# Moving the decays, the rings and the value loads of a two-layer encoder kernel

## The chip, the cores and the metric

The kernel runs on one core of one Trainium2 chip. The metric is device time in microseconds (us) of one execution; three executions of the kernel before are given below, and their median is what the prediction has to hit for the changed kernel. One further execution was recorded by the profiler, and every duration in this document that stands in a row comes from such a recorded execution.

## The reference

The program is one float32 encoder of two layers on 512 tokens of width 1024. Cut to what matters here:

```python
def _odd_mixer(x, norm_g, w_in, dec_f, dec_b, gn_g, w_out):
    h = _rmsnorm(x, norm_g)
    q, k, v, g = _split(h @ w_in, ODD_SPLITS)          # 1024, 1024, 2048, 2048 columns
    lgf = jax.nn.log_sigmoid(dec_f.astype(jnp.float32))   # 8 decays each way
    lgb = jax.nn.log_sigmoid(dec_b.astype(jnp.float32))
    y_f = _retention_dir(q, k, v, lgf, False)
    y_b = jnp.flip(_retention_dir(jnp.flip(q, 1), jnp.flip(k, 1), jnp.flip(v, 1), lgb, True), 1)
    ...                                                   # group norm per head -> yn
    return (jax.nn.silu(g) * yn) @ w_out

def reference(x, ...):
    for layer in range(DEPTH):
        x = x + (_even_mixer(x, ...) if layer % 2 == 0 else _odd_mixer(x, ...))
        x = x + _mlp(x, ...)                              # relu(h @ w1)**2 @ w2, 4096 wide
    return x
```

The even mixer is windowed attention with sinks beside neighbourhood attention on a grid. A retention head multiplies its scores by a decay per distance, `exp(log_gamma * distance)`; `log_gamma` is the log-sigmoid of 16 inputs.

## The kernel before, in words

Four stages follow each other on the one core: even mixer, first MLP, odd mixer, second MLP. Every float32 matmul is made of three products of rounded halves: an operand is split by a cast on ACT (the high part, `whi`, `shi`, `xh`, `uh`, `vh`) and a subtraction on DVE (the low part, `wlo`, `slo`, `xl`, `ul`, `vl`), and TensorE adds high·high, high·low and low·high. So each product waits for both a cast and a subtraction, and it can be late by either.

**Even mixer.** A scheduler with a cost model orders its instructions on every engine. Queries and keys are scaled by their norms (L464 on DVE; L460 and L465 on POOL), transposed by PE (L479), evacuated as high and low parts (L484, L494 on ACT, L485, L495 on DVE), and the window's scores (L635, L636 on PE) go through a fused minimum on DVE (L566) and an exponential on ACT (L576). `decays` (L1638) is called after the even mixer, and the scheduler is free to put its operations into gaps: they work on tiles of 128x16, most of them on POOL, and write `lg` and `nlb`, which the odd mixer reads some 600 us later.

**The MLPs and the odd mixer's values** are products of Strassen's kind. A *stream* is written in a fixed order for PE, DVE and ACT: at step k come the matmuls of block k, requests of weights (`ask`), the functions filed under `early[k]`, the cast of the weights of step k+2 (`high`, L1099), the functions under `mid[k]`, the subtraction for step k+2 (`low`, L1105), and those under `post[k]`. `request` (L1062) loads a block of 512 KB: blocks A12 and A22 into a ring of three (`wraw`), the others into a ring of six (`sraw`). S1 and S3 are sums of two blocks: SyncE's queue loads the first (L1068), and POOL issues an accumulating load of the second (L1070). `sum2` (L1077) makes S2 = A11 + S1 on DVE. `combine` (L999) makes the input sums of two of the eight row blocks: four operations on DVE into a tile `c` (L1009 to L1012), a cast `uh` (L1015), a subtraction `ul` (L1016).

**Start of the odd mixer.** The queries and keys of the first of four quarters are projected by `proj_a` (matmuls L186 to L188; its weights pass through the same ring `wraw`, with a cast L165 and a subtraction L166), evacuated by L1726 and L1731 and split by L1702 and L1703. Among that work stand the four `combine` calls, the first requests of the values' stream, and its first two `high` and `low`. The scheduler orders all of this too; only the stream behind it has a fixed order. The steps 0 and 1 of the stream take A11, 2 and 3 take S1, 4 and 5 S2, 6 and 7 A12, 8 and 9 S3; each is 12 matmuls of 512 columns (L1507 to L1509).

**Quarters.** Each of the four quarters has two heads. For quarter i: scores (L1788 to L1790), product with the decays (L1793), split into `ath`, `atl`, output (L1801 to L1803), then for each head the statistics of its group norm (cast L1819, subtraction L1820, two matmuls L1821 and L1822, then L1825 to L1827 on ACT and L1828, L1829 on DVE) and the gate (L1846, L1849, split into `zh`, `zl`), the output projection of the quarter before, and the projections of quarter i+1. In `project` each of the four value rows of the next quarter is loaded on ACT's queue (L1756) and split into `vh` (L1702) and `vl` (L1703). The scheduler orders this stage.

## Time and profile before

| what | value |
|---|---|
| three executions | 1300.21, 1300.35, 1302.45 us, median 1300.35 |
| profiled execution | 1302.67 us, of which 1300.9 us from the first to the last instruction (the span) |
| mean granted TensorE clock | 0.996 |
| busy, share of the span | PE 1277.1 us (98%), DVE 1055.0 (81%), ACT 825.6 (63%), POOL 152.2 (12%) |
| DMA | 196.15 MB, 151 GB/s over the span |

PE is busy nearly all the time, so what another engine does counts only where PE waits for it. A row of the waits reads: waiting engine, tile and line, then what it waited for, then total us, times, longest. A row of the timeline reads: start, duration, engine, line, operation, output and inputs, shape, count, and in brackets the idle time before it with what ended it. Matmuls overlap, so a row of PE is longer than its share: matmuls of 512 columns start 0.23 us apart at the full clock.

### The profile page before, as it was taken

To read this page: it belongs to the slowest core of one execution; us is meant where nothing else is said; L and a number is where in the kernel's file an instruction comes from. 1 tells how busy PE (TensorE), PEld (TensorE's weight loads), DVE (VectorE), ACT (ScalarE), POOL (GpSimd) and SP (SyncE) were. 2 spreads that over 40 slices of the span, in tenths; PEclk is the share of its full clock that TensorE was granted. 3 is DMA by queue.
4 is the path that set the end of the run, shared out by engine and by line. 5 is a ranking of instruction groups with operands and counts; after the bars stand their busy time and mean duration, and the time that the engine had idled before them with its cause. 6 is when DMAs were issued, how large, how long until landed. Compare 5 with 4: busy or idle time off the path is not lost.

```text
span 1300.9 us, 19400 instructions
## 1 busy us (share of the span) xinstructions
PE 1277.1 (98%) x7186; PEld 1117.9 (86%) x7186; DVE 1055.0 (81%) x1602; ACT 825.6 (63%) x1382; POOL 152.2 (12%) x169
## 2 busy tenths in 40 slices
PE   8899999999999999999999999999999999999998
PEld 7788978888989989887899977888888889898997
DVE  6588886959797997987888788877777787979888
ACT  4589875775766747675775566454547757566573
POOL 0322440001111101010110000000000111101100
PEclk9899999999999999999999999999999999999999
DMA  5222231758688686286899323415135777868862
GB/s 170 82 77 81 82 94 48 206 158 201 177 193 197 165 200 181 62 248 169 199 267 242 123 76 110 160 35 162 49 97 162 178 211 174 202 167 181 214 149 81
DMA packets 167072, 196.15 MB, mean 151 GB/s; under 512 B 12225, under 2 KB 124865, under 8 KB 166977
## 3 DMA queue, kind: packets, MB, share of 16 engines
q1 hardware_dynamic: 130384, 147.74, 36.7%
q0 software_dynamic: 27776, 37.75, 17.8%
q10 hardware_dynamic: 8816, 9.41, 2.3%
q8 instruction: 56, 0.92, 0.3%
q14 instruction: 40, 0.32, 0.1%
HBM read 184.39 MB, written 10.49 MB: 150 GB/s over the span
## 4 chain that ended last, share of the span: by engine, by line
PE 89%; DVE 5%; ACT 3%; DMA 1%; issue 1%; POOL 1%; SPq 0%; ACTq 0%; DVEq 0%; POOLq 0%
PE acc L1297 7%; PE acc L1298 7%; PE acc L1299 7%; PE acc L1313 7%; PE acc L1312 7%; PE acc L1314 7%; PE acc L186 7%; PE acc L188 6%; PE acc L187 6%; PE acc L1509 2%; PE acc L1508 2%; PE acc L1507 2%; PE aux L1297 1%; PE aux L1299 1%; PE aux L1298 1%
## 5 line engine op out<-in xcount | busy, mean ns | idle before, releaser
L1099 ACT CAST whi<-sraw 128x1024 fp32r<-128x1024 f32 x121 | 126.8, 1050 | 84.9 <-PE acc L1314 25.3
L1105 DVE TENSOR_TENSOR wlo<-sraw,whi 128x1024 fp32r<-128x1024 f32 x121 | 147.9, 1223 | 32.7 <-ACT whi L1099 32.2
L165 ACT CAST whi<-wraw 128x1024 fp32r<-128x1024 f32 (+2 forms) x83 | 78.4, 946 | 77.4 <-PE acc L187 38.8
L1070 POOL DMA_DIRECT2D sraw<-in_w_mlp_out_dram x32 | 38.7, 1236 | 625.9 <-DMA sraw<-in_w_mlp_out_dram 378.7
L166 DVE TENSOR_TENSOR wlo<-wraw,whi 128x1024 fp32r<-128x1024 f32 (+2 forms) x74 | 82.7, 1117 | 36.0 <-ACT whi L165 35.0
L186 PE MATMUL acc<-xh,whi 128*128 128x512 f32 x272 | 106.5, 392 | 0.0
L187 PE MATMUL acc<-xl,whi 128*128 128x512 f32 x272 | 106.1, 390 | 0.0
L188 PE MATMUL acc<-xh,wlo 128*128 128x512 f32 x272 | 105.6, 390 | 0.0
L1297 PE MATMUL acc<-uh,whi 128*128 128x256 f32 x344 | 97.8, 284 | 0.2
L1299 PE MATMUL acc<-uh,wlo 128*128 128x256 f32 x344 | 97.2, 283 | 0.0
L1298 PE MATMUL acc<-ul,whi 128*128 128x256 f32 x344 | 97.2, 283 | 0.0
L1099 ACT CAST shi<-sraw 128x1024 fp32r<-128x1024 f32 x59 | 62.1, 1052 | 38.8 <-PE acc L1314 10.7
L1105 DVE TENSOR_TENSOR slo<-sraw,shi 128x1024 fp32r<-128x1024 f32 x59 | 72.2, 1223 | 15.7 <-ACT shi L1099 15.4
L1266 DVE SCALAR_TENSOR_TENSOR rows<-acc,tok_r,rows 128x512 f32<-128x512 f32 (+1 forms) x97 | 71.8, 744 | 1.9 <-PE acc L1314 1.9
L1105 DVE TENSOR_TENSOR wlo<-wraw,whi 128x1024 fp32r<-128x1024 f32 x46 | 56.3, 1224 | 16.2 <-ACT whi L1099 16.2
L1297 PEld LDWEIGHTS acc<-uh,whi 128*128 128x128 f32 x344 | 65.6, 191 | 1.0 <-ACT s L1188 1.0
L1298 PEld LDWEIGHTS acc<-ul,whi 128*128 128x128 f32 x344 | 65.6, 191 | 0.0
L1299 PEld LDWEIGHTS acc<-uh,wlo 128*128 128x128 f32 x344 | 65.6, 191 | 0.0
L188 PEld LDWEIGHTS acc<-xh,wlo 128*128 128x128 f32 x272 | 51.0, 188 | 11.1 <-DVE wlo L166 0.4
L187 PEld LDWEIGHTS acc<-xl,whi 128*128 128x128 f32 x272 | 51.1, 188 | 10.5
L186 PEld LDWEIGHTS acc<-xh,whi 128*128 128x128 f32 x272 | 51.1, 188 | 10.5
L1099 ACT CAST whi<-wraw 128x1024 fp32r<-128x1024 f32 x46 | 48.3, 1051 | 12.5 <-PE acc L1314 8.9
(401 smaller groups left out, 4180.9 us busy)
## 6 DMA issues: line engine op xcount, KB each, us to landing
sraw<-in_w_mlp_out_dram SPq DMA_DIRECT2D x48, 512.0 KB
wraw<-in_w_mlp_in_dram SPq DMA_DIRECT2D x40, 512.0 KB
sraw<-in_w_mlp_in_dram SPq DMA_DIRECT2D x36, 512.0 KB
sraw<-in_w_mlp_out_dram POOLq DMA_DIRECT2D x32, 512.0 KB, 8.7
wraw<-in_w_mlp_out_dram SPq DMA_DIRECT2D x32, 512.0 KB
wraw<-in_w_in_o_dram SPq DMA_DIRECT2D x32, 512.0 KB
sraw<-in_w_mlp_in_dram POOLq DMA_DIRECT2D x24, 512.0 KB, 8.1
sraw<-in_w_in_o_dram SPq DMA_DIRECT2D x24, 512.0 KB
```

Of the source, the lines that this page charges most:

```text
L166: eng.tensor_tensor(lu, used, hu.bitcast(F32), op=ALU.subtract)
L186: mm(ps[m], hi[:, k % 4, cs], xh, start=k == 0, stop=False)
L187: mm(ps[m], hi[:, k % 4, cs], xl, start=False, stop=False)
L188: mm(ps[m], lo[:, k % 4, cs], xh, start=False, stop=k == nk - 1)
L1099: nc.scalar.copy(h, self.weight(k))
L1105: V.tensor_tensor(l, self.weight(k), h.bitcast(F32), op=ALU.subtract)
L1297: mm(o, h[:, i, cs], bh, start=st, stop=False, skip_group_check=True)
L1298: mm(o, h[:, i, cs], bl, start=False, stop=False, skip_group_check=True)
L1299: mm(o, l[:, i, cs], bh, start=False, stop=i == 3, skip_group_check=True)
L1312: mm(oc, bh[:, i, cs], hc, start=st, stop=False, skip_group_check=True)
L1313: mm(oc, bh[:, i, cs], lc, start=False, stop=False, skip_group_check=True)
L1314: mm(oc, bl[:, i, cs], hc, start=False, stop=end, skip_group_check=True)
```

## The change

Three edits, in the order of the program:

1. `decays` becomes a generator that is called in the first MLP's stream, at the steps 20 to 23, piece by piece. Two POOL operations become DVE operations; the clamped input goes into `lg` first.
2. In the values' stream the tile `c` no longer has a ring of its own (one slot) but takes slots in the ring `sraw` of six. The first requests are split: S1 and A11 after the second `combine`, A12 and then S3 after the projection of the keys. `sum2` of the first half is filed one step later.
3. The value rows of the next quarter are loaded by `load_v` right after both heads, and split by `split_v` after the first head's gate, no longer in `project`.

```diff
-        CB = ("c", 1)
-
...
             for q in range(2):
                 s = 14 * q
-                put(post, s - 2 if q else s, lambda q=q: self.sum2(2, q, 0))
-                put(post, s + 1, lambda q=q: self.sum2(2, q, 1))
+                put(post, s - 2 if q else s + 1, lambda q=q: self.sum2(2, q, 0))
+                put(post, s + 1 if q else s + 2, lambda q=q: self.sum2(2, q, 1))
...
     def decays():
         dx = hb[:, 8:24]
         u, s2, pl = ls
-        G.tensor_scalar(u, dx, -1.0, None, op0=ALU.mult)
-        V.tensor_tensor(u, u, dx, op=ALU.min)
+        V.scalar_tensor_tensor(u, dx, -1.0, dx, op0=ALU.mult, op1=ALU.min)
+        V.tensor_scalar(lg, dx, 0.0, None, op0=ALU.min)
+        yield
         act(u, u, AF.Exp)
-        G.tensor_scalar(s2, u, 2.0, None, op0=ALU.add)
+        yield
+        V.tensor_scalar(s2, u, 2.0, None, op0=ALU.add)
         V.reciprocal(s2, s2)
+        yield
         G.tensor_tensor(u, u, s2, op=ALU.mult)
...
-        V.tensor_scalar(u, dx, 0.0, None, op0=ALU.min)
         G.tensor_scalar(pl, pl, -2.0, None, op0=ALU.mult)
-        G.tensor_tensor(lg, pl, u, op=ALU.add)
+        G.tensor_tensor(lg, pl, lg, op=ALU.add)
...
                 if qt == 0:
                     values.combine(0)
-                    values.ask(-99, -2)
                     values.combine(1)
+                    values.ask(-99, -5)
                     values.combine(2)
                     values.combine(3)
                 proj_a(w_in_o, 0, 8, 1024 + qt * 256, xg, ev_k)
                 if qt == 0:
                     values.scales(rc)
-                    values.ask(-2, 0)
+                    values.ask(-2, 1)
+                    values.ask(-5, -2)
                     values.enter()
                     return
+                with tc.issue_after(mark):
+                    self.load_gates(nc.scalar)
+
+            def load_v(self):
+                self.back = []
                 for t in range(NB):
-                    r = row()
-                    with tc.issue_after(mark):
-                        if t == 0:
-                            self.load_gates(nc.scalar)
-                        nc.scalar.dma_start(r, scr[qt][t * P : (t + 1) * P, :])
-                    self.v[t] = split(r, "v", 4)
+                    self.back.append(row())
+                    with tc.issue_after(marks[-1]):
+                        nc.scalar.dma_start(
+                            self.back[t], scr[self.qt][t * P : (t + 1) * P, :]
+                        )
+
+            def split_v(self):
+                for t in range(NB):
+                    self.v[t] = split(self.back[t], "v", 4)
...
             q.head(0)
             q.head(1)
+            n and n.load_v()
             for c in range(2):
                 q.stats(c)
                 q.gate(c)
+                c == 0 and n and n.split_v()
                 p and p.output(4 * c, 4 * c + 4)
             n and n.project()
...
             st.enter()
+            if not last:
+                pieces = decays()
+                for k in range(20, 24):
+                    st.mid[k] = [lambda: next(pieces, None)]
...
     even_mixer(n_mlp0)
-    decays()
     mlp(0, n_mlp0(), n_odd)
```

The first place is POOL's list in the even mixer, before: the end of the first part of the decays (`ls`, `lg`, `nlb` are their tiles), scaling of queries (`qn`), a subtraction of weights, and the start of the second part.

```order
L1651 TENSOR_SCALAR ls_110<-ls_110 128x16
L1650 TENSOR_TENSOR ls_110<-ls_110,ls_109 128x16
L1651 TENSOR_SCALAR ls_110<-ls_110 128x16
L465 TENSOR_TENSOR qn<-raw,rs 128x4x64
L460 TENSOR_TENSOR qn<-raw,rs 128x512 x2
L166 TENSOR_TENSOR wlo<-wraw,whi 128x2x384
L465 TENSOR_TENSOR qn<-raw,rs 128x4x64
L1650 TENSOR_TENSOR ls_110<-ls_110,ls_109 128x16
L1651 TENSOR_SCALAR ls_110<-ls_110 128x16
```

In the changed kernel the same place of POOL's list reads:

```order
L96 TENSOR_SCALAR ngv<-gv 128x32
L465 TENSOR_TENSOR qn<-raw,rs 128x4x64
L460 TENSOR_TENSOR qn<-raw,rs 128x512 x2
L166 TENSOR_TENSOR wlo<-wraw,whi 128x2x384
L465 TENSOR_TENSOR qn<-raw,rs 128x4x64
L166 TENSOR_TENSOR wlo<-wraw,whi 128x2x384
```

The decays are gone from it (11 operations ahead of the first `qn` and 12 after the last), and so are three of them from DVE's list and one from ACT's; all other rows of the even mixer keep their order on PE, DVE, ACT and POOL.

The second place is SyncE's list at the start of the odd mixer, as a difference: `wraw ... 128x4x256` are the weights of the projections, `wraw` and `sraw ... 128x2x512` the blocks of the values' stream.

```order
 L144 DMA wraw<-in_w_in_o_dram 128x4x256 x4
+L1072 DMA wraw<-in_w_in_o_dram 128x2x512 x2
 L1068 DMA sraw<-in_w_in_o_dram 128x2x512 x2
 L1072 DMA sraw<-in_w_in_o_dram 128x2x512 x2
+L1072 DMA wraw<-in_w_in_o_dram 128x2x512
+L1068 DMA sraw<-in_w_in_o_dram 128x2x512 x4
```

The two blocks of A12 (`wraw`) moved ahead of S1 (L1068, `sraw`, two) and A11 (L1072, `sraw`, two), and S3 moved behind them. On DVE, at the same place, the second `low` of the values' stream (`wlo` of A11's second half, L1105) stood before like this:

```order
L1016 TENSOR_TENSOR ul_6288<-c_6282,uh_6287 128x1024
L1703 TENSOR_TENSOR ql_6271<-tmp_6268,qh_6270 128x512
L1703 TENSOR_TENSOR ql_6277<-tmp_6274,qh_6276 128x512
L1009 TENSOR_TENSOR c_6309<-row_6307 128x256
L1011 SCALAR_TENSOR_TENSOR c_6309<-xT3_6151,gv_76,row_6307 128x256
L1010 SCALAR_TENSOR_TENSOR c_6309<-xT3_6151,ngv_104,c_6309 128x256
L1105 TENSOR_TENSOR wlo_6424<-sraw_6299,whi_6423 128x1024
```

and in the changed kernel, from the first `low` (`slo`) on:

```order
L1105 TENSOR_TENSOR slo_6421<-sraw_6307,shi_6420 128x1024
L1016 TENSOR_TENSOR ul_6298<-c_6292,uh_6297 128x1024
L1016 TENSOR_TENSOR ul_6319<-c_6313,uh_6318 128x1024
L1009 TENSOR_TENSOR c_6324<-row_6322 128x256
L1011 SCALAR_TENSOR_TENSOR c_6324<-xT7_6158,gv_76,row_6322 128x256
L1010 SCALAR_TENSOR_TENSOR c_6324<-xT7_6158,ngv_104,c_6324 128x256
L1732 SCALAR_TENSOR_TENSOR tmp_6395<-acc_6333,rstd_b_6182 128x512
L1012 SCALAR_TENSOR_TENSOR c_6324<-xT7_6158,ngv_104,c_6324 128x256
L1732 SCALAR_TENSOR_TENSOR tmp_6401<-acc_6334,rstd_b_6182 128x512
L1704 TENSOR_TENSOR kl_6398<-tmp_6395,kh_6397 128x512
L1105 TENSOR_TENSOR wlo_6425<-sraw_6309,whi_6424 128x1024
```

That `low` moved from the second `combine` (`c_6309`) to behind the fourth (`c_6324`) and most of the evacuation of the keys.

The third place is PE's list between quarter 0 and quarter 1, where the statistics of head 1 (L1821, L1822; L1831, L1832 in the changed kernel) stand among the projection of quarter 1's queries. Before:

```order
L186 MATMUL acc_8241<-xh3_6057,whi_8244 128x512
L1821 MATMUL aux_8214<-ath_8215,ones_r_74 128x512
L187 MATMUL acc_8241<-xl3_6058,whi_8244 128x512
L188 MATMUL acc_8241<-xh3_6057,wlo_8245 128x512
L1822 MATMUL aux_8214<-atl_8216,ones_r_74 128x512
L186 MATMUL acc_8240<-xh4_6059,whi_8274 128x512
```

In the changed kernel:

```order
L1831 MATMUL aux_8237<-ath_8238,ones_r_74 128x512
L186 MATMUL acc_8263<-xh5_6060,whi_8297 128x512
L187 MATMUL acc_8263<-xl5_6061,whi_8297 128x512
L188 MATMUL acc_8263<-xh5_6060,wlo_8298 128x512
L186 MATMUL acc_8264<-xh5_6060,whi_8297 128x512
L187 MATMUL acc_8264<-xl5_6061,whi_8297 128x512
L188 MATMUL acc_8264<-xh5_6060,wlo_8298 128x512
L1832 MATMUL aux_8237<-atl_8239,ones_r_74 128x512
L186 MATMUL acc_8263<-xh6_6062,whi_8297 128x512
```

The second matmul of that pair is the 4305th of PE's list before and the 4317th now. The first matmul on the low part of the keys' weights (`wlo_8319` before, `wlo_8342` now) is the 4334th in both, so 29 matmuls stood between them and 17 do now. DVE makes that low part (L166) behind the same operations as before: what follows from the statistics (L1828, two `zl`, L1829).

## The prediction

> **What bounds the kernel now.** I read the page first, then the waits of PE, then the timelines around each wait, then the clock in windows.

> ```profile
> PE 1277.1 (98%) x7186; PEld 1117.9 (86%) x7186; DVE 1055.0 (81%) x1602; ACT 825.6 (63%) x1382; POOL 152.2 (12%) x169
> ...
> PE aux L635 <- DVE qk L485: 3.7, 1, 3.7
> ...
> PE acc L1508 <- DVE slo L1105: 2.0, 1, 2.0
> PE acc L186 <- ACT whi L165: 1.4, 1, 1.4
> ...
> PE acc L1509 <- DVE ul L1016: 1.0, 1, 1.0
> ...
> PE aux L1788 <- ACT kh L1702: 0.8, 1, 0.8
> ...
> PE aux L479 <- POOL qn L465: 0.3, 1, 0.3
> ```

> PE is the bound almost everywhere; it can only gain where it waits. The first five of these waits, at three places, are the ones that the three edits touch: one in the even mixer, two at the start of the values' stream, two between quarters 0 and 1. No matmul is removed. The third view shows what a wait costs beside its own length:

> ```profile
> 50.50:57.30 6.80, 5.66 (x21) 5.69 (x22) 4.92 (x12) 3.74 (x10) 0.00 (x0) 0.50 0.23 61
> ...
> 596.70:600.00 3.30, 3.30 (x9) 2.51 (x9) 1.70 (x2) 1.34 (x2) 1.59 (x2) 0.50 0.77 175
> 787.00:797.00 10.00, 8.31 (x35) 6.39 (x36) 9.76 (x16) 7.37 (x12) 0.00 (x0) 1.00 0.15 56
> ```

> The third figure from the right is the granted clock. It fell to half behind the wait in the even mixer, for 6.8 us, and behind the two of the values' stream (2.0 and 1.0 us, 2.3 us from one end to the other), for 3.4 us; behind the two between the quarters (0.8 and 1.4, 4.5 us from one end to the other) it stayed at 1.00. At half clock 3.4 us do the work of 1.7, so such a stretch costs 1.7 us more.

> **Edit 1, the decays.** What PE waits for in the even mixer is DVE, and DVE waits for POOL:

> ```profile
> 38.45 0.22 POOL L1646 TENSOR_TENSOR ls<-ls,ls 128x16 f32<-128x16 f32 x1 [0.93 <-DVE ls L1645]
> ...
> 41.34 0.62 POOL L465 TENSOR_TENSOR qn<-raw,rs 128x256 f32<-128x256 f32 x1
> ...
> 49.07 0.22 POOL L1652 TENSOR_TENSOR ls<-ls,ls 128x16 f32<-128x16 f32 x1
> ...
> 44.43 0.74 DVE L485 SCALAR_TENSOR_TENSOR qk<-aux,gq,qk 64x512 fp32r<-64x512 f32 x1 [0.25 <-ACT qk L484]
> 49.32 0.17 DVE L1653 TENSOR_SCALAR ls<-hb 128x16 f32<-128x16 f32 x1 [4.15 <-POOL ls L1652]
> ...
> 49.97 1.53 DVE L485 SCALAR_TENSOR_TENSOR qk<-aux,gq,qk 64x512 fp32r<-64x512 f32 x2
> ...
> 45.45 0.28 PE L636 MATMUL aux<-qk 128*128 128x256 f32 x1
> ...
> 47.65 0.34 PE L212 MATMUL acc<-whi,xl 128*128 128x384 f32 x1
> 51.64 0.55 PE L635 MATMUL aux<-qk 128*128 128x256 f32 x1 [3.65 <-DVE qk L485]
> ...
> 54.45 0.41 PE L635 MATMUL aux<-qk 128*128 128x256 f32 x1
> ...
> 57.39 0.33 PE L212 MATMUL acc<-whi,xl 128*128 128x384 f32 x1
> ```

> One tiny operation of the decays (L1653) sits in DVE's list ahead of the scores' minimum and the keys, and waits 4.15 us for POOL's polynomial. With it gone DVE takes the scores of 45.45 with L566 (0.5 us, from about 45.8) and L485 twice (1.5): done near 47.8, where PE comes to it at 47.8. POOL's chain from 38.45 no longer stands before L465 at 41.34, so PE's wait of 0.3 for it goes too, and PE and DVE both get there some 0.3 earlier, at 47.5. From 51.64 that is 4.1 us. The next L635, at 54.45, needs a fourth L485 (0.7) behind an L166 (1.0) on DVE: ready near 49.3, 5.1 us earlier than before, where PE would come without a wait near 48.9. From 54.45 to 57.39 PE runs 2.9 us at half clock; at the full clock it is 1.5 to 1.7. So the place of 57.39 comes at about 51.0: **-6.3 us**. Bounds: -3.7 if only the wait goes, -7.2 if the 0.4 at the fourth L485 doesn't come and PE gains 0.5 more ahead of it. I take the worked-out value, since the lists of PE and DVE are otherwise unchanged there.

> In the new place, the first MLP, the 21 POOL operations (nine of them take from 38.45 to 41.34, 0.32 us each: 6.7 us) stand between these two:

> ```profile
> 334.85 1.20 POOL L1070 DMA_DIRECT2D sraw<-in_w_mlp_out_dram  x1 [1.13 <-DMA sraw<-in_w_mlp_out_dram]
> 356.63 1.20 POOL L1070 DMA_DIRECT2D sraw<-in_w_mlp_out_dram  x1 [20.58 <-DMA sraw<-in_w_mlp_out_dram]
> ```

> 20.6 us idle cover them. The four operations on DVE and one on ACT (0.2 us each) lie in a stream where PE never waits: 0, and 1 us if that cover were gone.

> **Edit 2, the values' stream.** First what feeds it:

> ```profile
> 561.75 0.88 SPq L1068 DMA_DIRECT2D sraw<-in_w_in_o_dram  x2
> ...
> 564.95 9.56 SPq L1072 DMA_DIRECT2D wraw<-in_w_in_o_dram  x3
> ...
> 568.02 1.23 DVE L166 TENSOR_TENSOR wlo<-wraw,whi 128x1024 fp32r<-128x1024 f32 x1 [2.10 <-ACT whi L165]
> ...
> 564.00:588.00 24.00, 24.00 (x109) 19.79 (x108) 19.88 (x38) 16.61 (x26) 4.82 (x4) 1.00 1.07 292
> ```

> A12 takes slots of the ring that the projections' weights pass through; its second block can go out only when the L166 of 568.02 is done, at 569.2. In the changed queue S1 and A11 stand behind it: they go out at 569.2 and not from 561.75, 7.5 us later. At 292 GB/s a block of 512 KB takes 1.8 us. A12's second block, S1's two and A11's two are the first five, and S1's accumulating loads come between: A11's second block lands between 578.2 (five blocks) and 581.9 (seven), say 581.

> Then DVE. Its list behind the L166 of the last projection weights:

> ```profile
> 572.89 1.23 DVE L166 TENSOR_TENSOR wlo<-wraw,whi 128x1024 fp32r<-128x1024 f32 x1 [0.15 <-ACT whi L165]
> 574.03 1.28 DVE L1726 TENSOR_TENSOR tmp<-acc,rstd_b 128x512 f32<-128x512 f32 x2
> 575.23 1.22 DVE L1016 TENSOR_TENSOR ul<-c,uh 128x1024 fp32r<-128x1024 f32 x1
> 576.36 1.29 DVE L1703 TENSOR_TENSOR ql<-tmp,qh 128x512 fp32r<-128x512 f32 x2
> 577.56 0.42 DVE L1009 TENSOR_TENSOR c<-row 128x256 f32<-128x256 f32 x1
> ...
> 586.22 0.40 PE L1508 MATMUL acc<-wlo,xh 128*128 128x512 f32 x1
> ...
> 593.90 0.50 PE L1508 MATMUL acc<-slo,uh 128*128 128x512 f32 x1 [1.99 <-DVE slo L1105]
> ...
> 596.18 0.50 PE L1509 MATMUL acc<-shi,ul 128*128 128x512 f32 x1 [0.97 <-DVE ul L1016]
> ```

> From start to start: L166 and `low` 1.14, two L1726 1.20, L1016 1.13, two L1703 1.20; an operation of `combine` like L1009 0.4. Up to the first `low`: 1.14, 1.20, 1.13, 1.20, six operations of `combine` 2.4, `low` 1.13: done at 581.1. The second `low` then has two `ul` (2.3), four operations of `combine` (1.5), two evacuations and one `kl` (1.8) ahead of it, and itself 1.2: 587.9 at the earliest. The `uh` for the second `ul` stands on ACT behind the cast of A11's second block, so a landing at 581 adds about 0.7: 588.6. PE needs it at 586.22: a **new wait of 2.4 us**, and perhaps 0.2 on the next `low`. It is 1.7 without the landing, 4.8 if A11 lands 2.5 us later. What PE waited for at 593.90 and 596.18 (3.0 us) is not late any more, since three of the four `ul` are done before the stream's second step and PE comes 2.5 us later. A restart costs about 0.2 (an estimate: a row behind a wait is 0.50 long, the others 0.40, and the weights are loaded again). Lost before: 3.0, restarts 0.4, half clock 1.7: 5.1. Lost now: 2.6, restarts 0.4, and half clock 1.7 if a wait of this length brings it: 4.7. So **-0.4 us**, from -5.1 (no new wait at all) to +3.5 (the long one, and half clock twice).

> **Edit 3, the value rows.** The two waits between the quarters come from four casts `vh` on ACT that stand between `kh` and the weights:

> ```profile
> 782.23 2.15 ACTq L1756 DMA_DIRECT2D row<-values  x4
> ...
> 788.18 2.52 ACT L1702 CAST vh<-row 128x512 fp32r<-128x512 f32 x4 [0.31 <-DMA row<-values]
> ...
> 769.38 0.41 PE L1822 MATMUL aux<-atl,ones_r 128*128 128x512 f32 x1
> ...
> 774.90 1.22 DVE L166 TENSOR_TENSOR wlo<-wraw,whi 128x1024 fp32r<-128x1024 f32 x1
> ...
> 776.17 0.74 PE L188 MATMUL acc<-xh,wlo 128*128 128x512 f32 x2
> ```

> They move to the statistics, and both waits go: 2.2 and 0.4 of restarts, **-2.6 us**. The four loads move with them; their issue holds ACT for 2.2 us ahead of the last head's evacuation, where nothing of PE waits for it yet. But the casts and four `vl` of 0.6 on DVE push something too. Before, the chain from the second statistics matmul at 769.38 over ACT and DVE to the end of L166 at 776.1 takes 6.7 us, and 29 matmuls cover it (29 times 0.23 is 6.7): L188 at 776.17 comes just in time. In the changed list that matmul stands 12 later, near 772.15, and only 17 matmuls (3.9 us) cover the chain. Some 0.8 of the 6.7 were waits of ACT for a cast of weights and of DVE for a gate, so 5.9 are left: 772.15 + 5.9 is 778.05, needed at 776.05: a **new wait of 2.0 us**, at L188 for L166. It is nothing if the chain were hidden, 3.2 if the rows land late (they have 5 us from issue, as 782.23 to 788.18 took before) and the statistics matmul itself waits. Behind it `kl` and `ath` are late by 0.4 in sum, since another L166 stands between them on DVE. New: 2.0 + 0.4 + 0.4 of restarts, and half clock 1.7: **+4.5**. Net **+1.9 us**, from -2.6 to +3.5.

> **The clock.** The rows: 3.65 us of waiting brought half clock, 2.0 and 1.0 within 2.3 us brought it, 0.8 and 1.4 within 4.5 us did not. A single wait of 2.0 to 2.4 lies nearer to the second, so I count it both times. [...]

> **Sum.** -6.3 - 0.4 + 1.9 = **-4.8 us** against the profiled execution: 1302.67 becomes 1297.9, its span 1296.1. The median before is 2.3 us below the profiled execution, and I carry this over: 1300.35 - 4.8 = **1295.5**.

> **Rivals.**
> - *No half clock behind the new waits* (it seems to be counted over stretches of 3.4 us, and their border may cut a wait in two): -6.3 - 2.1 + 0.2 = -8.2, 1292.1. For: the full clock from 787 to 797. Against: 596.70. 0.22.
> - *At least one of the new waits isn't there.* Without that of edit 2 the sum is -6.3 - 5.1 + 1.9 = -9.5, without that of edit 3 -6.3 - 0.4 - 2.6 = -9.3, without both -14.0. So 1286.3 to 1291. For: DVE is busy 19.9 of the 24 us up to 588, so there is room. Against: the lists, which put the late operation last. 0.20.
> - *The gain of the even mixer is absorbed*: minimum, exponential and transposes, not PE, would set the pace behind 57, PE's waits there grow by what it gained, and -3.7 is left: sum -2.2, 1298.1. For: what PE waits for at 51.64 is such a chain. Against: no list is changed there. 0.15.
> - *Slower*: the requests behind A12 bring A11 so late that the stream starts dry. It decides when A11's second block lands at 587 and not 581: then the wait is 8.3 us with half clock twice, edit 2 costs +7.0, and the sum is +2.6, 1303. For: DMA is full up to 588. Against: only seven blocks are in the way. 0.04, and 0.03 for a weaker form that leaves no gain.
> - My forecast: 0.36, own range 1293 to 1298.

> A measurement tells 0.2% (2.6 us) from nothing. Faster, below 1297.75: the forecast but 0.01, the first two rivals, a third of the third: 0.82. Same: the rest of these and the weaker form of the last, 0.14. Slower: 0.04. The range that holds 8 in 10 is 1288.5 to 1298.5: it leaves out the case without both new waits and the late A11.

> **What would show it.** The wait of L635 gone and the clock 1.00 from 45 to 57; a wait L1506 or L1507 for `wlo` L1105 at the stream's second step, no wait for `slo` or `ul`; S1's requests behind a pause of SyncE; the waits at the first scores of quarter 1 and for `whi` gone, one of L188 for `wlo` L166 some 10 us before. I am wrong if the stream's second step starts without a wait, if the keys' L188 doesn't wait, or if the even mixer gives under 4 us.

## The result and the profile after

The changed kernel takes 1293.92 us (median of 1293.56, 1293.90, 1293.94 and 1295.38) beside 1300.28 us for the kernel before on the same chip: a ratio of 0.9949, 95% interval 0.9932 to 0.9967. Its profiled execution took 1295.38 us with a span of 1293.6, 7.3 us under that of before. Forecast were 1295.5 us, and 4.8 us less than before; measured are 6.4 us less between the medians and 7.3 between the profiled executions. The page's busy times and PE's waits of the changed kernel:

```profile
PE 1273.7 (98%) x7186; PEld 1115.5 (86%) x7186; DVE 1056.3 (82%) x1603; ACT 823.7 (64%) x1382; POOL 160.8 (12%) x167
...
PE acc L1506 <- DVE wlo L1105: 2.2, 1, 2.2
PE acc L188 <- DVE wlo L166: 2.1, 1, 2.1
...
PE acc L1297 <- ACT s L1188: 0.3, 1, 0.3
PE aux L635 <- DVE qk L485: 0.2, 1, 0.2
```

All five waits at which the edits aimed are gone or down to 0.2 us. The two new ones stand first in their places, where the prediction had put them: L1506 for `wlo` with 2.2 us (forecast 2.4) and L188 for `wlo` with 2.15 (forecast 2.0). L1297 is one that was not forecast. No wait of `kl` or `ath` came.

**Even mixer.** Windows, then the scores on PE, of the changed kernel:

```profile
44.00:57.00 13.00, 12.70 (x75) 11.24 (x75) 10.53 (x27) 11.01 (x26) 1.31 (x2) 1.00 0.35 95
```
```profile
47.28 0.36 PE L635 MATMUL aux<-qk 128*128 128x256 f32 x1
...
49.06 0.36 PE L635 MATMUL aux<-qk 128*128 128x256 f32 x1
```

These two stood at 51.64 and 54.45. They were forecast for 47.5 and 49.3, and the clock is 1.00 in the window.

**Start of the values' stream**: PE, then DVE, ACT and SyncE's queue in the changed kernel's timeline.

```profile
583.21 0.65 PE L1506 MATMUL acc<-wlo,xh 128*128 128x512 f32 x1 [2.22 <-DVE wlo L1105]
```
```profile
574.63 1.22 DVE L1105 TENSOR_TENSOR slo<-sraw,shi 128x1024 fp32r<-128x1024 f32 x1
...
581.34 0.68 DVE L1704 TENSOR_TENSOR kl<-tmp,kh 128x512 fp32r<-128x512 f32 x1
581.94 1.22 DVE L1105 TENSOR_TENSOR wlo<-sraw,whi 128x1024 fp32r<-128x1024 f32 x1
```
```profile
575.45 1.04 ACT L1099 CAST whi<-sraw 128x1024 fp32r<-128x1024 f32 x1
```
```profile
564.47 0.88 SPq L1068 DMA_DIRECT2D sraw<-in_w_in_o_dram  x2
565.40 0.98 SPq L1072 DMA_DIRECT2D sraw<-in_w_in_o_dram  x2
```

S1 and A11 go out at 564.5 to 566.4, which in the clock of before (5.4 us later) is 569.9 and on: forecast 569.2. A11's second block is there by 575.45, when its cast runs; its subtraction comes 5.4 us after that cast, behind DVE's other work up to `kl`. The wait is DVE's.

**Quarter 0 to 1**, PE in the changed kernel:

```profile
765.53 0.40 PE L1832 MATMUL aux<-atl,ones_r 128*128 128x512 f32 x1
...
771.70 0.73 PE L188 MATMUL acc<-xh,wlo 128*128 128x512 f32 x2 [2.15 <-DVE wlo L166]
```

From the statistics' matmul to L188 6.2 us pass; forecast were 5.9.

**Where the time went**, stage by stage. The same matmul of PE's 7186 is compared in two traces, and the columns give how much later (+) or earlier (-) it comes than in the profile of before: at number 130 (33 us in), and then what each stage adds up to numbers 1000, 2800, 4150, 5000. Half clock counts the stretches of 3.41 us at a granted clock of 0.50 up to PE's last matmul, from the stage of the column in which they fall (E even mixer, V values' stream, Q quarters).

| kernel | start | even mixer | first MLP | values' stream | quarters 0 to 1 | half clock |
|---|---|---|---|---|---|---|
| before, profile of the result | 0 | 0 | 0 | 0 | 0 | E 2, V 1 |
| before, second profile | -0.27 | -2.38 | -0.05 | +0.97 | -0.63 | V 2 |
| changed, profile of the result | +0.31 | -6.18 | +0.48 | -1.14 | -0.77 | V 1 |
| changed, second profile | +0.62 | -6.36 | +0.44 | -1.44 | +0.98 | V 1, Q 1 |
| changed, third profile | +0.10 | -6.29 | +0.39 | -3.09 | +0.92 | Q 1 |
| edit 1 alone | +0.38 | -6.20 | +0.41 | -0.27 | -0.83 | V 1 |
| edit 2 alone | +0.34 | +0.29 | -0.06 | -2.86 | -0.40 | E 2 |
| edit 3 alone | -0.19 | -0.28 | -0.05 | +0.04 | -0.69 | E 2, V 1 |
| split late | +0.04 | -6.06 | +0.40 | -1.31 | -2.20 | V 1 |
| subtractions first, both | -0.19 | -6.16 | +0.44 | -2.99 | +0.90 | Q 1 |
| subtractions first, one | -0.46 | -6.18 | +0.39 | -2.68 | +0.89 | Q 1 |
| decays at 35 to 38 | +0.14 | -6.32 | -0.06 | -0.79 | -0.67 | V 1 |
| no polynomial | -0.69 | -6.08 | +0.36 | -2.78 | +0.96 | Q 1 |
| three edits together | +0.08 | -5.98 | -0.06 | -2.48 | -2.17 | none |

Behind number 5000 no kernel changes by more than about 0.1.

The profile of before in the first row is one draw, not a fixed mark. The kernel before, unchanged, takes 2.4 us less in the even mixer in its second profile, where no half clock came in that stage, and 1.0 more in the values' stream, where half clock lasted two stretches. The quarters take 0.4 to 0.8 less than in the first row in all three profiles without edit 3 (the second of before, edit 1 alone, edit 2 alone), since the old wait for `whi` was longest in the first row: 1.4 us there, 0.8, 0.7 and 1.1 in these. Of the second of before:

```profile
PE acc L186 <- ACT whi L165: 0.8, 1, 0.8
```

### The profile page after: what moved, and what is told of

Read it like the earlier page. It is cut to its first block, busy times and chain, and to the rows that moved or that the text cites. A ratio compares the mean times of both kernels' runs of the same rounds, so it can differ in the third digit from the quotient of the medians.

```text
span 1293.6 us, 19405 instructions
## 1 busy us (share of the span) xinstructions
PE 1273.7 (98%) x7186; PEld 1115.5 (86%) x7186; DVE 1056.3 (82%) x1603; ACT 823.7 (64%) x1382; POOL 160.8 (12%) x167
## 4 chain that ended last, share of the span: by engine, by line
PE 81%; DVE 8%; ACT 7%; issue 2%; DMA 1%; POOL 0%; SPq 0%; ACTq 0%; DVEq 0%
PE acc L1313 7%; PE acc L1314 7%; PE acc L1312 7%; PE acc L188 6%; PE acc L186 6%; PE acc L187 6%; PE acc L1297 5%; PE acc L1298 5%; PE acc L1299 5%; PE acc L1506 2%; PE acc L1507 2%; PE acc L1505 2%; DVE wlo L1105 1%; PE aux L1811 1%; PE aux L1812 1%
## 5 line engine op out<-in xcount | busy, mean ns | idle before, releaser
L1105 DVE TENSOR_TENSOR wlo<-sraw,whi 128x1024 fp32r<-128x1024 f32 x121 | 147.8, 1221 | 34.5 <-ACT whi L1099 33.8
L165 ACT CAST whi<-wraw 128x1024 fp32r<-128x1024 f32 (+2 forms) x83 | 78.6, 947 | 85.4 <-PE acc L187 48.6
L1070 POOL DMA_DIRECT2D sraw<-in_w_mlp_out_dram x32 | 38.7, 1242 | 601.3 <-DMA sraw<-in_w_mlp_out_dram 372.4
L166 DVE TENSOR_TENSOR wlo<-wraw,whi 128x1024 fp32r<-128x1024 f32 (+2 forms) x74 | 82.6, 1116 | 37.2 <-ACT whi L165 36.3
L188 PE MATMUL acc<-xh,wlo 128*128 128x512 f32 x272 | 105.7, 390 | 2.1 <-DVE wlo L166 2.1
L186 PE MATMUL acc<-xh,whi 128*128 128x512 f32 x272 | 106.5, 392 | 0.0
L1297 PE MATMUL acc<-uh,whi 128*128 128x256 f32 x344 | 97.8, 284 | 0.5 <-ACT s L1188 0.3
L1105 DVE TENSOR_TENSOR slo<-sraw,shi 128x1024 fp32r<-128x1024 f32 x59 | 72.0, 1221 | 16.3 <-ACT shi L1099 15.9
L1105 DVE TENSOR_TENSOR wlo<-wraw,whi 128x1024 fp32r<-128x1024 f32 x46 | 56.1, 1219 | 15.5 <-ACT whi L1099 15.5
L1297 PEld LDWEIGHTS acc<-uh,whi 128*128 128x128 f32 x344 | 65.6, 191 | 1.5 <-ACT s L1188 1.5
L188 PEld LDWEIGHTS acc<-xh,wlo 128*128 128x128 f32 x272 | 51.0, 188 | 13.2 <-DVE wlo L166 2.6
L186 PEld LDWEIGHTS acc<-xh,whi 128*128 128x128 f32 x272 | 51.1, 188 | 10.4
```

The costliest lines, as they stand in the source:

```text
L166: eng.tensor_tensor(lu, used, hu.bitcast(F32), op=ALU.subtract)
L186: mm(ps[m], hi[:, k % 4, cs], xh, start=k == 0, stop=False)
L188: mm(ps[m], lo[:, k % 4, cs], xh, start=False, stop=k == nk - 1)
L1105: V.tensor_tensor(l, self.weight(k), h.bitcast(F32), op=ALU.subtract)
L1297: mm(o, h[:, i, cs], bh, start=st, stop=False, skip_group_check=True)
```

## The experiments

### Each edit alone

Edit 1 is the hunk on `decays` with its call at the steps 20 to 23; edit 2 `CB`, `sum2` and the `ask` calls; edit 3 `load_v` and `split_v`. Each was put into the kernel before by itself:

```diff
 # edit 1
-    decays()
+                for k in range(20, 24):
+                    st.mid[k] = [lambda: next(pieces, None)]
 # edit 2
-        CB = ("c", 1)
-                    values.ask(-99, -2)
+                    values.ask(-99, -5)
 # edit 3
+            n and n.load_v()
+                c == 0 and n and n.split_v()
```

> The kernel before with edit 1 alone (the decays in the first MLP's stream; rings and value loads as before). Theory, edits that add up: in the even mixer the wait of L635 for L485 goes and the clock stays at 1.00, 5.9 us behind that stage as in the profile of the kernel with all edits; in the first MLP 0.5 us are lost where the decays now stand; sum -5.4 us, about 1294.9. The waits of the values' stream (2.0 and 1.0) and between the quarters (0.8 and 1.4) stay. Rival, the sizes of the prediction: -6.3 and nothing lost in the MLP, 1294.0. Second rival, edits that lean on each other: under 4 us alone, above 1296.3.

Measured: 1297.29 us beside 1301.87 for the kernel before on this chip, ratio 0.9969 (0.9957 to 0.9981). Even mixer -6.2, first MLP +0.4. So edit 1 does alone what it does with the others, and most of the gain comes from it (0.31 of 0.51% by the ratios). The theory's 1294.9 was missed by 2.4 us, and 1297.29 lies in the range that the second rival had named. But the kernel before took 1.6 us more on this chip, and the medians differ by 4.6 us, where the theory had 5.4 and that rival under 4. So the time alone does not separate the two. The stages of the profile do: they show no sign of edits that lean on each other. The table counts from matmul 130, so that a start that differs by 0.3 from execution to execution doesn't enter; without that the even mixer read -5.9.

> The kernel before with edit 2 alone (input sums in the ring of six, requests split, first sum one step later). Theory: the waits for slo and ul (3.0 us) go, one of 2.2 us of L1506 for wlo L1105 comes; -1.1 us if half clock follows it as it followed the old ones, about 1299.2; about -2.8, 1297.5, if the clock stays up this time, which it would where the border of a 3.41 us stretch cuts the wait so that under 1.7 us of it lie in one. Rival, the size of the prediction: -0.4 with half clock. Second rival: no new wait without the other two edits, -5, 1295.3.

Measured: 1299.79 us, ratio 0.9983 (0.9974 to 0.9992). The old waits are gone, and L1506 waits 1.9 us for `wlo`. Of the theory's two cases the second came in the profile: no half clock in the stream, -2.9. Its condition was not met, though: 1.86 us of the wait lay in one stretch (PE busy for 1.55 of 3.41, last section), where it had under 1.7 as its estimate. The new wait needs no other edit.

> The kernel before with edit 3 alone (value rows of the next quarter loaded after the heads, split behind the first head's gate). Theory: the waits of 0.8 and 1.4 us for kh and whi go, one of 2.15 us of L188 for wlo L166 comes; -0.7 us at full clock behind it, about 1299.6, or +1.0, 1301.3, where the whole wait lies in one of the clock's 3.41 us stretches and half clock follows. Rival, the prediction: half clock follows a wait of this length always, +1.0 to +1.9. Second rival: no wait at L188, -2.6, 1297.7.

Measured: 1302.06 us, ratio 1.0003 (0.9994 to 1.0012): no difference that can be measured. In the profile L188 waits 2.1 us, the clock stays at 1.00 behind it, and the quarters take 0.7 less than in the first profile of before, but so do the three profiles without edit 3 named above (0.4 to 0.8 less); the spread from 1300.5 to 1302.9 is as wide as that of the kernel before. The three ratios together give -0.45%, all edits at once -0.51%: within the intervals they add up.

### The value rows split later

```diff
-                c == 0 and n and n.split_v()
+                c == (i == 0) and n and n.split_v()
```

> The changed kernel, but in quarter 0 the value rows are split behind the second head's gate and not the first's; loads as in the changed kernel. Theory: L188 waits because four casts vh on ACT and four vl on DVE push the second head's statistics behind; with them later the statistics' matmuls stand 11 earlier in PE's list, the wait of 2.15 us goes or falls under 0.5, and nothing waits for kh or whi, since two of the casts are still done before: -1.5 to -2.2 us against the changed kernel, 1291.8 to 1292.4. Rival A: the chain of statistics, not the casts, is what L188 waits for: the wait stays within 0.5 us of 2.15, 1293.9. Rival B: the late casts bring back the waits of before at kh and whi (up to 2.2 us): 1293.9, with other waits.

Measured: 1291.87 us (1290.97 to 1293.95), ratio 0.9928 (0.9916 to 0.9941). PE in this kernel, then DVE:

```profile
761.92 0.40 PE L1831 MATMUL aux<-ath,ones_r 128*128 128x512 f32 x1
762.61 0.40 PE L1832 MATMUL aux<-atl,ones_r 128*128 128x512 f32 x1
...
775.25 0.73 PE L188 MATMUL acc<-xh,wlo 128*128 128x512 f32 x2 [0.69 <-DVE wlo L166]
```
```profile
763.99 1.22 DVE L166 TENSOR_TENSOR wlo<-wraw,whi 128x1024 fp32r<-128x1024 f32 x1
...
773.97 1.22 DVE L166 TENSOR_TENSOR wlo<-wraw,whi 128x1024 fp32r<-128x1024 f32 x1
```

The statistics' matmul comes 11 places earlier in PE's list, and the wait of 2.15 is gone: the low part of the keys' first weights is made at 763.99 and not, as in the changed kernel, at 770.43. The wait of 0.69 (the expectation had under 0.5) is another one, 24 matmuls later: PE now comes earlier to the keys' second weights, whose low part is made at 773.97 (774.09 in the changed kernel). Nothing waits for `kh` or `whi`, so rival B falls, and the quarters take 1.4 less than in the changed kernel at full clock. The edit moves nothing but the place of the split, so that place sets the wait. How it does so is not shown in full: on DVE the first L166 now also stands ahead of the second head's statistics, which the theory did not have. Rival A's size (a wait within 0.5 us of 2.15) falls; what the chain of statistics has to do with it was not taken apart.

### The stream's first subtractions earlier on DVE

```diff
         def enter(self):
             self.high(0); self.low(0)
-            self.high(1)
-            self.low(1)
+            with tc.high_priority(40):      # 80 in the second kernel
+                self.high(1)
+                self.low(1)
```

> The changed kernel with the values' stream's second cast and subtraction, and those filed behind them, at a higher priority in the scheduler: DVE's L1105 for step 1 and step 2 now stand ahead of both key evacuations' kl (L1704), on ACT both kh stand behind the stream's casts. PE's list is the same. Theory, DVE's order sets the wait of 2.2 us and A11 has long landed (its cast ran at 575.45): step 1 has its wlo at 581.0 and does not wait, step 2 has its own at 583.7 where PE comes at 583.8, and the third slo is up to 0.6 us late at step 3. Wait of 2.2 becomes 0 to 0.7 and half clock goes: -1.7 to -2.2 us without half clock's share, 1291.7 to 1292.2, and up to 1.7 less where the changed kernel's executions had half clock. Rival, the landing sets it: the wait stays at 2.0 to 2.4, 1293.9.

> The changed kernel with the subtraction L1105 of step 1 alone moved up, four operations and two evacuations earlier on DVE; everything that DVE has to do ahead of step 2 stays. Theory, it is the amount of DVE's work ahead of the stream and not one operation's place: the wait at step 1 goes and one of 1.3 to 1.9 us comes at step 2, since its wlo is done near 585.5 and PE comes at 583.8; net -0.3 to -0.9 us against the changed kernel in PE's positions. Rival, the place of that one operation alone: no wait at either step, -2.2.

Measured: 1295.72 us, ratio 0.9959 (0.9945 to 0.9972), for the first; the second, with one execution, 1295.62. PE's waits in this stage, of the first kernel and then of the second:

```profile
586.38 0.50 PE L1506 MATMUL acc<-slo,uh 128*128 128x512 f32 x1 [0.33 <-DVE slo L1105]
...
589.93 0.50 PE L1506 MATMUL acc<-wlo,uh 128*128 128x512 f32 x1 [0.54 <-DVE wlo L1105]
...
593.48 0.50 PE L1506 MATMUL acc<-wlo,uh 128*128 128x512 f32 x1 [0.50 <-DVE wlo L1105]
```
```profile
583.44 0.50 PE L1506 MATMUL acc<-wlo,uh 128*128 128x512 f32 x1 [0.54 <-DVE wlo L1105]
```

In the second kernel waits of 0.55 and 0.49 follow at 589.86 and 593.41, as in the first; the 1.3 to 1.9 expected at its step 2 are 0.54.

The wait of 2.2 is gone in both, so it was DVE's order and not the landing of A11 that set it: that rival falls. But my expected gain fell too. The stream takes -3.0 and -2.7 here, at full clock; the changed kernel takes -3.1 in its third profile, at full clock and with a wait of 1.7. What was one wait became three of 0.3 to 0.55, 1.4 to 1.6 us in sum, and only the half clock behind it was saved. Behind the first steps stands a chain that PE overtakes once it no longer starts late, in DVE's and ACT's rows of the first kernel:

```profile
586.25 1.21 DVE L1077 TENSOR_TENSOR sraw<-sraw 128x1024 f32<-128x1024 f32 x1
588.65 1.22 DVE L1105 TENSOR_TENSOR wlo<-sraw,whi 128x1024 fp32r<-128x1024 f32 x1 [1.19 <-ACT whi L1099]
589.79 1.22 DVE L1077 TENSOR_TENSOR sraw<-sraw 128x1024 f32<-128x1024 f32 x1
```
```profile
587.57 1.05 ACT L1099 CAST whi<-sraw 128x1024 fp32r<-128x1024 f32 x1 [3.64 <-DVE sraw L1077]
```

Sum, cast and subtraction of a block follow each other, and the next sum comes 3.54 us after the first, while PE needs 2.8 (12 matmuls of 0.23). The second sum is what edit 2 files one step later; whether filing it earlier would help wasn't tried. The medians lie above the changed kernel's, but the ratio's interval overlaps that of the changed kernel, so the two are not told apart. The profiles show two things on the losing side: half clock at L188, which two of the changed kernel's three profiles have too, and an end of the program that is 1.0 us longer (last section).

### The decays' new place

```diff
-                for k in range(20, 24):
+                for k in range(35, 39):
```

> The changed kernel with the decays' pieces at the steps 35 to 38 of the first MLP's stream (products of the second matrix, where ACT idles 1.6 us a step) and not 20 to 23. Theory: the 0.48 us that PE lost in the MLP came from five operations of 0.2 us in a chain of ACT and DVE without slack; at the new steps nothing waits: -0.4 to -0.5 us in PE's positions, 1293.4. Rival: POOL's polynomial beside DVE costs it, wherever it stands: the 0.5 stays.

```diff
         yield
-        G.tensor_tensor(u, u, s2, op=ALU.mult)
-        ...
-        G.tensor_tensor(lg, pl, lg, op=ALU.add)
         G.tensor_scalar(nlb, lg[:, 8:16], -1.0, None, op0=ALU.mult)
```

> The changed kernel without the decays' polynomial: 20 of the 21 POOL operations are left out, so the decays are not log-sigmoids but only the clamped inputs; the operations on DVE and ACT stay at the steps 20 to 23. Theory: the 0.48 us in the first MLP stay, since the small operations on DVE and ACT cause them. Rival: POOL causes them, and they go.

Measured: at the steps 35 to 38 the first MLP loses nothing (-0.06 for +0.48); without the polynomial it still loses 0.36. The median of the former, 1294.25 (ratio 0.9945, 0.9931 to 0.9959), doesn't tell 0.5 us apart. Weight loads of before and then of the changed kernel at the place, and the changed kernel's DVE and ACT there:

```profile
352.81 0.19 PEld L1297 LDWEIGHTS acc<-uh,whi 128*128 128x128 f32 x1 [0.24 <-ACT s L1188]
```
```profile
341.15 0.19 PEld L1297 LDWEIGHTS acc<-uh,whi 128*128 128x128 f32 x1 [0.24 <-ACT s L1188]
347.44 0.19 PEld L1297 LDWEIGHTS acc<-uh,whi 128*128 128x128 f32 x1 [0.47 <-ACT s L1188]
```
```profile
341.01 0.17 DVE L1645 TENSOR_SCALAR ls<-ls 128x16 f32<-128x16 f32 x1
341.21 0.26 DVE L1646 RECIPROCAL ls<-ls 128x16 f32<-128x16 f32 x1
```
```profile
336.62 0.21 ACT L1643 ACTIVATE ls<-ls 128x16 f32<-128x16 f32 x1
...
340.52 0.58 ACT L1188 COPY s<-acc 128x512 f32<-128x512 f32 x1
```

In the kernel before the evacuation L1188 ended just when PE needed it the first time, and 0.24 us late the second time (352.81, the same load as 347.44). In the changed kernel both come 0.23 to 0.24 later, which together is the 0.48 that the stage lost. The operations on DVE and ACT are what is left as the cause, since at the steps 35 to 38 the loss is gone and without the polynomial 0.36 of it stays; up to 0.1 may be POOL's. The weight loads' rows showed that this place had no slack, where PE's row of waits showed nothing.

### Three edits together, and the same kernels again

The late split, the subtractions at priority 40 and the decays at 35 to 38 in one kernel; then the changed kernel twice more, and the kernel before once more, unchanged.

> The changed kernel with three of the earlier edits together: in quarter 0 the value rows split behind the second gate, the stream's second cast and subtraction at the higher priority of the first of the two such kernels, the decays at the steps 35 to 38. Theory, the gains add up as the single kernels showed them in PE's positions: -1.3 (quarters), -0.7 without and -2.4 with half clock's share (values' stream; 1.3 of waits at the steps 3 and 4 and of restarts stay), -0.5 (first MLP); and as no wait of 1.9 us or more is left outside the even mixer, no half clock in any execution. About -4 against an execution of the changed kernel with one half clock, 1290 to 1291, and a smaller spread between executions. Rival, the waits lean on each other (what is gained at the stream is lost at the next wait of the odd mixer): -2 or less, 1292 and above.

Measured: 1291.39 us beside 1300.76 for the kernel before (four of six executions from 1291.21 to 1291.41, the others 1293.16 and 1293.77), ratio 0.9933 (0.9919 to 0.9947). No half clock in the profile; PE's last matmul comes 3.3 us earlier than in the changed kernel's first profile. The median lies below those of both kernels, but the kernels were timed on different chips, and the ratio's interval overlaps that of the changed kernel, and that of the late split alone. The quarters and the first MLP gave what they had given alone; at the stream the total is +0.6 against the changed kernel's third profile where -0.7 was expected: four waits of 0.2 to 0.55 us stand there, as in the kernels with the subtractions first. The median misses the 1290 to 1291 that were expected by 0.4 and lies under the rival's 1292. And without half clock two executions still lie 2 us above the others: that part of the spread is not explained.

> The changed kernel unchanged, one more execution with a profile. Theory: the clock is judged over stretches of 3.41 us whose borders lie differently in each execution; half clock follows a stretch in which PE waited 1.9 us or more, and no other. So of the waits of 2.2 (values' stream) and 2.15 us (quarters) each is followed by half clock exactly where 1.9 us of it lie between two borders. Rival, as the prediction had it: the length of the wait alone decides, so the pattern of the first profile comes again: half clock behind the first wait, none behind the second.

> The changed kernel unchanged, a third execution with a profile; expected as for the second: half clock by where the borders lie (theory), or the same pattern in each (rival).

> The kernel before, one more execution with a profile. Theory: half clock always behind the wait of 3.65 us in the even mixer, since no border leaves less than 1.9 us of it in both neighbours unless it cuts it in the middle; behind the waits of 2.0 and 1.0 us in the values' stream only where the borders leave 1.9 us of them in one stretch. Rival: the same pattern as in the first profile, half clock behind both.

Measured: 1296.89, 1294.68 and 1300.39 us. Windows cut at the borders of the clock's stretches (taken every 3.413 us from where the clock is seen to change; last section); the third figure from the right is the clock, and PE's busy time stands behind the length. The changed kernel's first profile, its second, its third, and the second of before:

```profile
579.99:583.41 3.42, 1.20 (x6) 0.68 (x5) 3.42 (x6) 2.95 (x4) 0.44 (x1) 1.00 0.43 146
583.41:586.82 3.41, 3.41 (x9) 2.63 (x9) 3.41 (x4) 0.67 (x2) 0.76 (x1) 0.50 0.52 69
767.72:771.14 3.42, 1.83 (x9) 1.17 (x7) 3.13 (x5) 2.24 (x4) 0.00 (x0) 1.00 0.00 0
771.14:774.55 3.41, 2.85 (x13) 2.36 (x13) 3.41 (x6) 0.95 (x2) 0.00 (x0) 1.00 0.43 142
```
```profile
580.45:583.86 3.41, 1.53 (x7) 0.98 (x6) 3.41 (x5) 2.79 (x4) 0.69 (x1) 1.00 0.32 120
583.86:587.27 3.41, 3.41 (x10) 2.63 (x9) 3.41 (x5) 0.59 (x1) 0.51 (x1) 0.50 0.64 80
768.19:771.60 3.41, 1.26 (x7) 0.72 (x6) 3.41 (x6) 1.55 (x3) 0.00 (x0) 1.00 0.00 0
771.60:775.01 3.41, 3.41 (x9) 2.63 (x10) 3.41 (x5) 1.22 (x2) 0.00 (x0) 0.50 0.48 157
```
```profile
579.57:582.98 3.41, 1.71 (x8) 1.09 (x7) 3.41 (x5) 2.97 (x4) 0.15 (x1) 1.00 0.39 139
582.98:586.39 3.41, 3.41 (x16) 2.60 (x15) 3.41 (x5) 0.59 (x1) 1.04 (x1) 1.00 0.49 87
767.32:770.73 3.41, 1.42 (x6) 1.20 (x7) 3.41 (x6) 0.25 (x1) 0.00 (x0) 1.00 0.07 14
770.73:774.14 3.41, 3.41 (x10) 2.64 (x9) 3.41 (x6) 1.22 (x2) 0.00 (x0) 0.50 0.77 242
```
```profile
46.07:49.48 3.41, 1.59 (x10) 1.27 (x8) 0.50 (x2) 0.02 (x1) 2.56 (x12) 1.00 0.43 115
49.48:52.90 3.42, 1.59 (x11) 1.38 (x11) 3.29 (x6) 2.64 (x5) 0.36 (x2) 1.00 0.01 2
```

One kernel, three profiles, three patterns. The same wait of 2.15 us at L188 is cut by a border in the first (1.59 us of it fall into one stretch, PE is busy for 1.83, the clock stays) and lies whole or nearly whole in one stretch in the others (PE busy 1.26 and 1.42, half clock next). In the kernel before even the wait of 3.65 us in the even mixer was once cut in two equal parts and brought no half clock: 2.4 us less in that stage. In the same profile half clock behind the waits of 2.0 and 0.8 us in the values' stream lasted two stretches, against one in the first. So the rival, the length alone, falls; my own expectation that the even mixer's wait always brings it falls too, but for the case of the cut in the middle that it named. The theory's 1.9 us is no sharp limit: half clock came behind a stretch with 1.88 us of waiting (second profile, PE busy for 1.53) and, in the first profile of before, behind one with 1.65 (593.22 to 596.63, PE busy for 1.76).

## Why the prediction came out as it did

The median was forecast within 1.6 us, and the waits that went and came are those forecast. Part of the closeness is luck: the profiled execution came out 2.5 us below its forecast (1295.38 for 1297.9), and the median lies only 1.5 us below the profiled execution, where the prediction carried over 2.3 from the kernel before. Most of the 2.5 is half clock that did not come behind L188 (1.7); the rest are the terms below. They are measured against the first profile of before, as the prediction was:

- **Edit 1, -6.3:** -6.2, right, with the rows at 47.28 and 49.06. It is the value against a profile of before with half clock in the even mixer, as three of the four profiles with the decays still there have it; against the second profile of before, which has none, it is 3.6 to 4.0, and the medians with edit 1 alone differ by 4.6. The cost of the new place was put at 0 because PE never waits there; it was 0.4 to 0.5. The POOL operations were put at 6.7 us under an idle time of 20.6; they took 15.6 (341.6 to 357.2), and POOL's next request went out at 357.13, some 6 us later than in the kernel without the polynomial (349.85, in a trace that runs 1 us ahead). Nothing waited for that.
- **Edit 2, -0.4:** -1.1 to -1.4 with half clock, -3.1 without. The wait was 2.2 for 2.4 (1.7 to 2.5 in the other profiles); the 0.2 at the next subtraction did not come, and the stage's total leaves no room for the restarts' 0.4.
- **Edit 3, +1.9:** -0.8 at full clock and +0.95 with half clock. The old waits were put at 2.6. By the late split, whose quarters take 2.2 less with 0.69 of waiting left, they cost 2.9 in this profile of before, but 2.1 to 2.5 in the three other profiles without edit 3. Against those, edit 3 brings nothing to 0.4 at full clock and costs 1.3 to 1.8 with half clock. Of the new waits 2.15 came and none of the 0.4 for `kl` and `ath`; the total leaves no room for the restarts' 0.4.
- **Half clock counted behind both new waits:** this is the term that was mis-sized. In the prediction it was a matter of the wait's length. By the profiles it is, for waits of this length, a matter of where a border falls: behind L1506 half clock came in 4 of 7 profiles that have this wait at 1.7 to 2.5 us, behind L188 in 5 of 8 that have 2.1 us there. Some 0.6 of the 1.7 (an estimate from these counts) would have been the value to take, twice. With both half clocks, as forecast, the changed kernel took 1296.89 in the one execution that shows them.

The first rival (no half clock, 1292.1) is thus the other half of the same gamble, and my reason for it, borders that may cut a wait, was the right one: at L188 half clock came where PE was busy for 1.26 and 1.42 us of a stretch and stayed away where a border left it 1.83. The four timed executions lie between its 1292.1 and the forecast's 1295.5. The even mixer's gain was not absorbed, no new wait was missing, and A11 was in time.

## What to carry to other kernels

Work moved off a wait belongs where the receiving engines have slack in their own chain, not where PE's row shows no wait: five operations of 0.2 us cost 0.4 to 0.5 us in one place of the MLP and nothing 15 steps later. When one operation is late, add up what its engine has to do before the next two or three deadlines; if the list is too long, a better order only splits the wait. And in these profiles a wait of PE of about 2 us had two prices, with and without a stretch of 3.41 us at half clock (the quarters at +0.98 and -0.77 in the changed kernel's second and first profile, with a wait of 2.1 at L188 in both): where the profiles of a kernel show both, count the mean of both, and take several profiles before reading one.

## What the runs showed of the hardware

```profile
587.00:590.41 3.41, 1.55 (x7) 1.32 (x8) 3.41 (x5) 2.26 (x4) 1.19 (x1) 1.00 0.11 41
```
```profile
767.55:770.96 3.41, 1.52 (x7) 0.94 (x5) 3.41 (x5) 1.93 (x3) 0.00 (x0) 1.00 0.00 0
```

The other two with half clock both had the two waits of the old values' stream in them: 593.22 to 596.63 in the profile of before (PE busy 1.76) and 592.50 to 595.91 with edit 3 alone (1.57). A stretch that was itself at half clock was followed by another one where PE was busy in it for 2.27 us (50.50 to 53.91 in the profile of before) and for 2.57 (592.20 to 595.61 in its second), and by full clock where PE was busy all through it (53.91 to 57.32 and 596.63 to 600.04 in the profile of before). Matmul ends in a trace are modelled, so a border of some tenths is what can be said. In the kernel before the spread of the times goes with this: over 42 executions of the kernel before on three chips, those with a mean clock of 0.998 took 1298.2 to 1298.5 us, those with 0.997 1299.6 to 1301.6, those below 1301.7 to 1303.3. In the changed kernel it does not: its executions at 0.998 took 1293.9, the one at 0.999 took 1295.38, and the mean clock also counts half clock behind PE's last matmul, which costs nothing (in the profile of before that matmul starts at 1296.65, and the clock is at half from 1299.78 on).

**POOL's tiny operations took longer beside some of DVE's.** In the even mixer of before, while DVE waited, they took 0.22 to 0.25 us each (46.48 to 48.98); in the changed kernel:

```profile
341.63 0.99 POOL L1648 TENSOR_TENSOR ls<-ls,ls 128x16 f32<-128x16 f32 x1 [11.74 <-DVE ls L1646]
342.70 1.07 POOL L1649 TENSOR_TENSOR ls<-ls 128x16 f32<-128x16 f32 x1
...
344.46 0.22 POOL L1652 TENSOR_TENSOR ls<-ls,ls 128x16 f32<-128x16 f32 x1
```
```profile
341.38 1.16 DVE L1082 TENSOR_TENSOR sraw<-sraw,wraw 128x1024 f32<-128x1024 f32 x1
342.46 1.23 DVE L1105 TENSOR_TENSOR slo<-sraw,shi 128x1024 fp32r<-128x1024 f32 x1
```

The first two end at 342.62 and 343.77, within 0.1 of the ends of the DVE operations that run beside them (342.54 and 343.69). The two DVE operations took 1.16 and 1.23 us, where L1105 took 1.22 in the mean of the whole program. POOL's row of 344.46 took 0.22 with another operation of DVE beside it (L1192, 344.24 to 344.92). What held the first two back was not shown.

**The end of the program differs by kernel.** From PE's last matmul to the end of the span pass 3.9 us in all five profiles of the kernels before and changed, but 4.3 to 5.0 in six of the nine others (5.0 in the combined one). So 1.1 of the 3.3 us that PE gained there came back. In the traces of five of these six an instruction fetch lands within the last half microsecond, and in none of the traces with an end of 3.9; whether that is the cause wasn't tried.
